# Last quarter of the output stage of a decoder layer: ScalarE and GpSimd in written order, weight columns two tiles ahead and gates one tile ahead

## The chip, the core and the metric

The kernel is one program on one core of a Trainium2 chip. Its time is the device time of one execution in microseconds (us); lower is better. The core's engines have queues of their own and each runs its queue in order: TensorE (PE in the rows, its weight loads PEld), VectorE (DVE), ScalarE (ACT), GpSimd (POOL) and SyncE (SP), which issues most of the DMAs. GpSimd issues DMAs too, from the same queue as its arithmetic.

## What is computed

One decoder layer on 2048 tokens of width 1024, in float32. Cut to the part around the change:

```python
y_a = sliding_window_attention(...) @ w_attn_out     # (T, 512) @ (512, 1024)
y_b = gated_delta_rule(...)         @ w_dn_out       # (T, 512) @ (512, 1024)
merged = sigmoid(g_a) * y_a + sigmoid(g_b) * y_b
x = layer_norm(ALPHA * x + merged @ w_out)
x = layer_norm(ALPHA * x + square(relu(x @ w_up)) @ w_down)
```

## The kernel before, in words

**Stages.** A first stage projects the input and runs attention and the delta rule, and leaves in DRAM the two mixer outputs (`ya_d`, `yb_d`) and tanh of half the gates (`tg_d`). Then comes the output stage, the one that the change touches (about 1166 to 1533 us of the execution). An up stage (L1403 is its matmul) and a down stage (L1525) follow. Every matmul operand is split in a high and a low part, so a product takes three matmuls per block of 128.

**The output stage** runs over four quarters of 512 tokens (`q`, L1021). A quarter has two halves:

- The column half, L1029 to L1066: eight tiles `m` of 128 output columns. `y_weights(m)` (L1008) loads the columns `m` of both weights through SP (L1015, L1016) and splits them on ScalarE (L110, high part) and VectorE (L111, low part). Two products of 12 matmuls each (L147) fill one PSUM bank each out of six. VectorE multiplies each bank with (1 + gate) (L1063), adds the two (L1064), ScalarE rounds the sum to the high part `mgh` (L1065) and VectorE takes the low part `mgl` (L1066). The two gate tiles of `m` come by two DMAs of GpSimd (L1035) into a ring of six places, so a load for tile `m` waits until tile `m`-3 has been used up.
- The row half, L1089 to L1112: `merged @ w_out` for four blocks of 128 rows (matmul L1110), with the residual added by VectorE (L1112).

**What rides along.** The four row blocks of quarter `q` are normalised during the column half of quarter `q`+1, one each at `m` = 1 to 4 (L1046 to L1049): statistics on VectorE (L872 to L876), the reciprocal root on GpSimd (L877), two passes on VectorE (L881, L883), and a store that GpSimd issues (L884). Three tiles later, at `m` = 4 to 7, the block is transposed (`turn_rows`, L1000): eight transposes on PE (L1004) into two PSUM banks, two copies out on ScalarE (L1006) into two buffers `xt`, two stores that GpSimd issues (L1007). PE's order is the order of the program text throughout.

**In the last quarter only**, `x_sums` (L894) prepares the first half of the up stage's input: four chunks of 1 MB, each a load that GpSimd issues (L899), four subtractions on GpSimd (L888, L889, L891, L892) and a store that GpSimd issues (L902). Two steps of it are taken per tile (L1055 to L1057): the first step ends the chunk before (L891, L892, store) and issues the next load, the second does L888 and L889 on what that load brings. After the column half the row loads (L1078) and the first operands of the up stage (L946, L951, L954) are issued.

**What sets the order.** Outside a `manual_schedule` region, a planner at compile time orders each engine's queue by its own model of readiness and by priority. Inside a region, the engines named keep the order of the program text. PE is in one from the start; the row half of the last quarter has one for VectorE and ScalarE (L1081); the up and down stages have one for VectorE, ScalarE, GpSimd and SP. The column half has none for ScalarE and GpSimd, so the planner may put loads, sums and roots where it likes.

```python
            for m in range(NK):
                gates = []
                for i in range(2):
                    th = tgs[:, tgn % 6, :]
                    tgn += 1
                    if q > 0 or m > 2:
                        lastg = G.dma_start(th, tg_d[q][:, i * NK + m, :])
                    gates.append(th)
...
                if lastq:
                    next(sums, None)
                    next(sums, None)
                wh, wl = wy or y_weights(m)
```

Of the kernel before, what the change touches and what calls it, by code (L numbers as in the profile page):

```python
# [10 lines left out]
AF = mybir.ActivationFunctionType  # L11
ALU = mybir.AluOpType
# [3 lines left out]
P = 128  # L16
T = 2048
D = 1024
NK = D // P
TQ = 512  # L20
# [25 lines left out]
def hybrid_layer(ctx: ExitStack, tc: tile.TileContext, x, w_in, conv_w, sinks, a_log, dt_bias, norm_w,  # L46
                 w_attn, w_dn, w_out, ln1_g, ln1_b, w_up, w_down, ln2_g, ln2_b, out):
    nc = tc.nc
    V, A, G, PE = nc.vector, nc.scalar, nc.gpsimd, nc.tensor
# [103 lines left out]
    with ExitStack() as st:  # L153
# [4 lines left out]
        ps = pool(st, "a_ps", space=PSUM)  # L158
# [705 lines left out]
    def layer_norm(*args, **kw):  # L864
        for _ in norm_steps(*args, **kw):
            pass
# [102 lines left out]
    with ExitStack() as st:  # L969
        sb = pool(st, "b_sb")  # L970
        ps = pool(st, "b_ps", space=PSUM)

        def prepare(q):
            ys = []
            for i, src in enumerate((ya_d[q], yb_d[q])):
                t = xslot(2 * (q % 2) + i)
                yh, yl = t[:, 0], t[:, 1]
                for hf in range(2):
                    hs = slice(2 * hf, 2 * hf + 2)
                    raw = stage[:, 2 * i + hf]  # L980
                    if q == 0:
                        with tc.high_priority(offset=HP):
                            loads.append(nc.sync.dma_start(raw, src[:, hs, :]))
                    else:
                        G.dma_start(raw, src[:, hs, :])
                    split(raw, yh[:, hs, :], yl[:, hs, :])
                ys.append((yh, yl))
            return ys

        stage = xslot(5, (4, 2, TQ), F32)  # L990
        turned = []
        loads = []
        ready = prepare(0)
        V.memset(mh, -0.5)
        tgs = xslot(4, (8, TQ), F32)
        tgn = 0

        def turn_rows(r, t):

            s, th, tb = t // 8, t // 4 % 2, t % 4  # L1000
            for kh in range(2):
                ps_ = acc_bank((P, 4, P))
                for k in range(4):
                    PE.transpose(ps_[:, k, :], r[:, (kh * 4 + k) * P:(kh * 4 + k + 1) * P], ident)  # L1004
                xt = new(sb, [P, 4, P], "xt", 2)
                A.activation(xt, ps_, AF.Copy)  # L1006
                G.dma_start(x1t_d[s][:, kh, th, :, tb * P:tb * P + P], xt)  # L1007

        def y_weights(m):
            ms = slice(m * P, (m + 1) * P)  # L1010

            def load_y(raw):
                wa = w_attn.rearrange("(j t d) c -> j d t c", j=2, t=4)
                for j in range(2):
                    nc.sync.dma_start(raw[64 * j:64 * j + 64, 0:4, :], wa[j][:, :, ms])  # L1015
                loads.append(nc.sync.dma_start(raw[:, 4:8, :], w_dn[:, ms].rearrange("(k p) c -> p k c", p=P)))  # L1016

            with (tc.issue_after(loads[-1].ins) if len(loads) < 20 else nullcontext()):
                return weights(None, [NK, P], load=load_y)

        for q in range(NQ):  # L1021
            t0 = q * TQ
            ys = ready
            lastq = q == NQ - 1
            mgh = xslot(6, (NK, TQ))
            mgl = new(sb, [P, NK, TQ], "mgl", 1, F32R)
            if q == NQ - 1:
                sums = x_sums(0, lambda c: stage[:, 2 * (c % 2):2 * (c % 2) + 2].rearrange("p a b t -> p (a b) t"), TQ)
            for m in range(NK):  # L1029
                gates = []  # L1030
                for i in range(2):
                    th = tgs[:, tgn % 6, :]
                    tgn += 1
                    if q > 0 or m > 2:
                        lastg = G.dma_start(th, tg_d[q][:, i * NK + m, :])  # L1035
                    gates.append(th)
                wy = y_weights(m) if q == 0 else None
                if q == 0 and m < 3:
                    with tc.issue_after(loads[-1].ins):
                        for i, th in enumerate(gates):  # L1040
                            loads.append(nc.sync.dma_start(th, tg_d[q][:, i * NK + m, :]))
                if q == 0 and m == 6:
                    with tc.issue_after(lastg.ins):
                        G.dma_start(gt, ln1_g[0].partition_broadcast(P))
                        G.dma_start(bt_, ln1_b[0].partition_broadcast(P))
                if m > 0 and norms:  # L1046
                    r, t = norms.pop(0)
                    layer_norm(r, gt, bt_, mh, x1_d[t])
                    turned.append((r, t, m + 3))  # L1049
                if turned and turned[0][2] <= m:  # L1050
                    turn_rows(*turned.pop(0)[:2])
                if m == 4 and not lastq:
                    with tc.issue_after(lastg.ins):
                        ready = prepare(q + 1)
                if lastq:  # L1055
                    next(sums, None)
                    next(sums, None)  # L1057
                wh, wl = wy or y_weights(m)
                for i in range(2):
                    yh, yl = ys[i]  # L1060
                    pp = new(ps, [P, TQ], "b", 6)
                    product(pp, wh, wl, [yh], [yl], 4, 4 * i)
                    V.scalar_tensor_tensor(gates[i], gates[i], 1.0, pp, ALU.add, ALU.mult)  # L1063
                V.tensor_tensor(gates[0], gates[0], gates[1], ALU.add)  # L1064
                A.activation(mgh[:, m, :], gates[0], AF.Copy, scale=0.5)  # L1065
                V.scalar_tensor_tensor(mgl[:, m, :], gates[0], 0.5, mgh[:, m, :], ALU.mult, ALU.subtract)  # L1066
            while turned:
                turn_rows(*turned.pop(0)[:2])
            early = iter(("B11", "T1", "T2", "T3", "B21")) if lastq else iter(())
            ne = 0  # L1070
            if lastq:
                for _ in sums:
                    pass
            rt = []
            for tb in range(4):
                r = row_tile()
                with tc.issue_after(lastg.ins):
                    G.dma_start(r, rows(t0 + tb * P))  # L1078
                rt.append(r)

            with tc.manual_schedule(engines={V.engine, A.engine}) if lastq else nullcontext():  # L1081
                def out_weights(n):
                    ch, kk = divmod(n, 4)
                    cs = slice(ch * 512, ch * 512 + 512)
                    return weights(w_out[kk * 256:kk * 256 + 256, cs].rearrange("(k p) c -> p k c", p=P), [2, 512])

                ready_w = [out_weights(0), out_weights(1)]
                begun = []
                for ch in range(2):  # L1089
                    cs = slice(ch * 512, ch * 512 + 512)  # L1090
                    accs = [new(ps, [P, 512], "b", 6) for _ in range(4)]
                    for kk in range(4):
                        wh, wl = ready_w.pop(0)
                        if ch * 4 + kk + 2 < 8:
                            ready_w.append(out_weights(ch * 4 + kk + 2))
                        for steps in begun:
                            run(steps)
                        begun = []
                        name = next(early, None)
                        if name:  # L1100
                            with tc.issue_after(lastg.ins):
                                begun.append(x_operand(0, name, xops[0], [flat(stage[:, 2 * (ne % 2) + i]) for i in range(2)], G))
                                next(begun[0])
                            ne += 1
                        for tb in range(4):
                            ts_ = slice(tb * P, tb * P + P)
                            for k in range(2):
                                kg = 2 * kk + k
                                for n, (a, b) in enumerate(((mgh, wh), (mgh, wl), (mgl, wh))):
                                    PE.matmul(accs[tb], lhsT=a[:, kg, ts_], rhs=b[:, k, :], start=kg == 0 and n == 0, stop=kg == 7 and n == 2)  # L1110
                    for tb in range(4):
                        V.scalar_tensor_tensor(rt[tb][:, cs], rt[tb][:, cs], ALPHA, accs[tb], ALU.mult, ALU.add)  # L1112
            for tb in range(4):
                norms.append((rt[tb], q * 4 + tb))
# [472 lines left out]
```

## Time and profile before

| | |
|---|---|
| median of three runs | 2804.24 us (2802.61 to 2807.36) |
| the profiled execution's own time | 2804.84 us |
| its span, first to last instruction | 2803.1 us |
| PE busy over the span | 2736.3 us (98%) |
| VectorE, ScalarE, GpSimd busy | 1910.8, 1198.7, 691.5 us |
| column half of the last quarter | 1435.0 to 1489.3 us |

The rows of the profile further down are of a few kinds. A timeline row gives the start in us, the duration in us, the engine, the line, the operation, what is written and read, how many instructions were merged, and in brackets how long the engine was idle before and what ended that. A windows row gives a stretch and, for each engine, its busy time and instructions, then the granted TensorE clock as a share of full speed, the DMA engines' busy share and GB/s. A source view is about one line of the kernel: its instructions with minimum, median and maximum duration in ns, who waited for them, and for a DMA the time from issue to landing.

### The profile page before, as it was taken

The page shows a single profiled execution, that of the slowest core. Times are in us where ns is not written, and L with a number is a line of the kernel's source. Part 1 is how long each engine was busy: PE and PEld are TensorE (multiplying, and loading weights), DVE is VectorE, ACT ScalarE, POOL GpSimd, SP SyncE. Part 2 cuts the span into 40 slices and gives each one's busy share as a digit, 9 for nine tenths or more (in the row PEclk, how much of TensorE's full clock was granted, in tenths as well). Part 3 has the DMA queues.
Part 4 walks back from the last instruction along what each step waited for, and adds up shares of the span by engine and source line. Part 5 has one row for each costly group of instructions (what it writes and reads, how often), then busy time and mean ns, then how long its engine had stood idle before and what let it go on. Part 6 is the DMA issues. An engine that isn't in the chain of part 4 may idle for free.

```text
span 2803.1 us, 37882 instructions
## 1 busy us (share of the span) xinstructions
PE 2736.3 (98%) x13509; PEld 2258.8 (81%) x13509; DVE 1910.8 (68%) x3034; ACT 1198.7 (43%) x2400; POOL 691.5 (25%) x915
## 2 busy tenths in 40 slices
PE   8999999999999999999999999999999999999996
PEld 6878888888888888888878888878887788888875
DVE  6875666456636673566757866688866777777778
ACT  4545443444344434433324555565555332223344
POOL 1022302230223032213452124458830000000015
PEclk9999999999999999999999999999999999999998
DMA  6785546444635464867787677788976644444443
GB/s 215 233 278 192 210 169 213 136 176 169 211 133 192 158 202 143 235 214 266 251 275 254 192 225 233 245 284 296 301 240 210 233 157 148 132 133 148 146 143 139
DMA packets 356045, 569.92 MB, mean 203 GB/s; under 512 B 42273, under 2 KB 236945, under 8 KB 355857
## 3 DMA queue, kind: packets, MB, share of 16 engines
q1 hardware_dynamic: 315056, 428.54, 47.1%
q0 software_dynamic: 40800, 138.96, 14.2%
q8 instruction: 107, 1.75, 0.3%
q14 instruction: 82, 0.66, 0.1%
HBM read 391.22 MB, written 176.19 MB: 202 GB/s over the span
## 4 chain that ended last, share of the span: by engine, by line
PE 83%; DVE 7%; DMA 4%; issue 2%; ACT 2%; POOL 1%; SPq 0%; DVEq 0%; ACTq 0%; POOLq 0%
PE pj L329 25%; PE X L1403 12%; PE X L1525 11%; PE Z L1403 6%; PE Z L1525 5%; PE b L1110 5%; PE b L147 5%; PE Y L1403 3%; PE Y L1525 3%; PE d L554 2%; DMA w<-in_w_in_dram 1%; DVE prod L542 1%; DVE qs L543 1%; PE at L779 1%; PE d L488 1%
## 5 line engine op out<-in xcount | busy, mean ns | idle before, releaser
L329 PE MATMUL pj<-x,w 128*128 128x512 f32 x3648 | 930.3, 399 | 4.6 <-DVE qs L723 2.1
L329 PEld LDWEIGHTS pj<-x,w 128*128 128x128 f32 x3648 | 662.1, 189 | 129.0 <-issue 2.5
L1525 PE MATMUL X<-x,w 128*128 128x512 f32 x1536 | 370.1, 394 | 11.9 <-DVE st L1487 7.8
L1403 PE MATMUL X<-x,w 128*128 128x512 f32 x1536 | 366.6, 391 | 6.2 <-ACT c L1359 5.0
L1525 PEld LDWEIGHTS X<-x,w 128*128 128x128 f32 x1536 | 290.0, 190 | 77.4 <-issue 15.0
L1403 PEld LDWEIGHTS X<-x,w 128*128 128x128 f32 x1536 | 288.7, 188 | 68.3 <-ACT c L1359 6.3
L1232 ACT ACTIVATE w<-w 128x1024 fp32r<-128x1024 f32 x96 | 101.5, 1059 | 258.9 <-DMA w<-h 253.6
L1403 PE MATMUL Z<-x,w 128*128 128x512 f32 x768 | 184.9, 390 | 0.0
L1525 PE MATMUL Z<-x,w 128*128 128x512 f32 x768 | 184.5, 389 | 0.0
L1146 DVE TENSOR_TENSOR w<-w,w 128x512 fp32r<-128x512 f32 x224 | 175.4, 794 | 9.2 <-ACT w L1142 9.2
L147 PE MATMUL b<-x,w 128*128 128x512 f32 x768 | 179.9, 393 | 0.5 <-DVE x L1063 0.5
L111 DVE TENSOR_TENSOR w<-w,w 128x1024 fp32r<-128x1024 f32 x102 | 125.7, 1232 | 79.8 <-PE b L1110 44.7
L110 ACT ACTIVATE w<-w 128x1024 fp32r<-128x1024 f32 x102 | 107.8, 1057 | 161.4 <-DMA w<-in_w_dn_out_dram 90.9
L147 PEld LDWEIGHTS b<-x,w 128*128 128x128 f32 x768 | 144.0, 189 | 30.7 <-DVE x L1063 0.9
L1525 PEld LDWEIGHTS Z<-x,w 128*128 128x128 f32 x768 | 144.1, 188 | 29.9
L1403 PEld LDWEIGHTS Z<-x,w 128*128 128x128 f32 x768 | 143.9, 188 | 29.9
L1475 DVE SCALAR_TENSOR_TENSOR x<-x,X 128x1024 f32<-128x1024 f32 x96 | 117.0, 1219 | 62.3 <-PE X L1525 62.3
L1110 PE MATMUL b<-w,x 128*128 128x512 f32 x512 | 157.6, 389 | 0.0
L1142 ACT ACTIVATE w<-w 128x512 fp32r<-128x512 f32 x224 | 135.9, 621 | 48.3 <-DVE w L1152 26.8
L1488 POOL TENSOR_TENSOR st<-st,mh 128x1 f32<-128x1 f32 x12 | 6.5, 552 | 580.8 <-DVE st L1487 580.8
L1236 DVE TENSOR_TENSOR w<-w,w 128x1024 fp32r<-128x1024 f32 x96 | 123.0, 1282 | 13.6 <-ACT w L1232 13.5
L414 DVE SCALAR_TENSOR_TENSOR acc<-cin,cw,acc 128x512 f32<-128x512 f32 x144 | 114.8, 797 | 15.9 <-ACT acc L412 13.6
(326 smaller groups left out, 4351.4 us busy)
## 6 DMA issues: line engine op xcount, KB each, us to landing
w<-whd SPq DMA_DIRECT2D x114, 512.0 KB, 3.3
w<-wld SPq DMA_DIRECT2D x114, 512.0 KB, 4.6
h<-c SPq DMA_DIRECT2D x224, 256.0 KB, 4.3
w<-h SPq DMA_DIRECT2D x96, 512.0 KB, 3.5
w<-in_w_up_dram SPq DMA_DIRECT2D x64, 512.0 KB, 5.8
w<-in_w_in_dram SPq DMA_DIRECT2D x38, 512.0 KB, 4.4
whd<-w SPq DMA_DIRECT2D x38, 512.0 KB, 3.0
wld<-w SPq DMA_DIRECT2D x38, 512.0 KB, 5.0
```

The source lines that it names most:

```text
L110: A.activation(hi, raw, AF.Copy)
L111: V.tensor_tensor(lo, raw, hi, ALU.subtract)
L147: PE.matmul(pp, lhsT=a[:, k0 + k, :], rhs=b[k // 4][:, k % 4, :], start=n == 0, stop=n == 3 * nk - 1)
L329: PE.matmul(pp, lhsT=a[:, k, :], rhs=b[k // 4][:, k % 4, :], start=n == 0, stop=n == 23)
L414: V.scalar_tensor_tensor(acc, cin[:, j:j + TQ], cw[:, 12 * j + gi:12 * j + gi + 1], acc, ALU.mult, ALU.add)
L1110: PE.matmul(accs[tb], lhsT=a[:, kg, ts_], rhs=b[:, k, :], start=kg == 0 and n == 0, stop=kg == 7 and n == 2)
L1142: A.activation(t[:, 0, :], src, AF.Copy)
L1146: V.tensor_tensor(l, raw[name], h, ALU.subtract)
L1236: V.tensor_tensor(parts[1], raw_, parts[0], ALU.subtract)
L1403: PE.matmul(dst, lhsT=l[:, ks], rhs=r[:, xs], start=first and k == 0 and m == 0, stop=k == 3 and m == 2, skip_group_check=not first)
L1475: V.scalar_tensor_tensor(dst, dst, 1.0 if (tq, half, ch) in touched else ALPHA, bank, ALU.mult, ALU.add)
L1525: PE.matmul(dst[:, j], lhsT=l[:, ks], rhs=r[:, k], start=first and k == 0 and m == 0, stop=k == 1 and m == 2, skip_group_check=not first)
```

## The change

In the last quarter alone the column half is put in a `manual_schedule` region for ScalarE and GpSimd, so that both keep the order of the program text there, DMA issues of GpSimd included. To suit that order, `y_weights` is written two tiles ahead and the gate loads one tile ahead. No operation is added or taken away. The other quarters keep their text and the planner's order.

```diff
-            for m in range(NK):
+            def load_gates(m):
+                nonlocal tgn, lastg
                 gates = []
                 for i in range(2):
                     th = tgs[:, tgn % 6, :]
...
                         lastg = G.dma_start(th, tg_d[q][:, i * NK + m, :])
                     gates.append(th)
+                return gates
+
+            with tc.manual_schedule(engines={A.engine, G.engine}) if lastq else nullcontext():
+                coming = [y_weights(0), y_weights(1)] if lastq else []
+                gates_of = [load_gates(0)] if lastq else []
+                for m in range(NK):
+                    if lastq:
+                        if m + 1 < NK:
+                            gates_of.append(load_gates(m + 1))
+                        gates = gates_of.pop(0)
+                    else:
+                        gates = load_gates(m)
...
+                    if m > 0 and norms:
+                        r, t = norms.pop(0)
+                        layer_norm(r, gt, bt_, mh, x1_d[t])
+                        turned.append((r, t, m + 3))
+                    if turned and turned[0][2] <= m:
+                        turn_rows(*turned.pop(0)[:2])
...
+                    if lastq:
+                        next(sums, None)
+                        next(sums, None)
+                    if lastq:
+                        if m + 2 < NK:
+                            coming.append(y_weights(m + 2))
+                        wy = coming.pop(0)
+                    wh, wl = wy or y_weights(m)
...
+                        V.scalar_tensor_tensor(gates[i], gates[i], 1.0, pp, ALU.add, ALU.mult)
+                    V.tensor_tensor(gates[0], gates[0], gates[1], ALU.add)
+                    A.activation(mgh[:, m, :], gates[0], AF.Copy, scale=0.5)
+                    V.scalar_tensor_tensor(mgl[:, m, :], gates[0], 0.5, mgh[:, m, :], ALU.mult, ALU.subtract)
```

## Rows read from the trace of the kernel before

**Rows 1.** Windows view, this column half: PE, PEld, DVE, ACT, POOL, clock, DMA.
```profile
1435.00:1489.30 54.30, 49.41 (x226) 40.46 (x225) 39.65 (x54) 16.41 (x22) 32.58 (x39) 0.97 0.86 277
```

**Rows 2.** The chain that ended last: eight tiles of the first quarter without a pause.
```profile
1165.94 43.58 PE b L147 x192
```

**Rows 3.** Timeline of PE in the last quarter's column half.
```profile
1435.00 19.25 PE L147 MATMUL b<-x,w 128*128 128x512 f32 x84
...
1468.48 1.56 PE L1004 MATMUL pj<-ident,r 128*128 128x128 f32 x8 [4.38 <-ACT xt L1006]
1469.69 7.04 PE L147 MATMUL b<-x,w 128*128 128x512 f32 x24
...
1482.94 1.04 PE L1004 MATMUL pj<-ident,r 128*128 128x128 f32 x8
1483.73 5.69 PE L147 MATMUL b<-x,w 128*128 128x512 f32 x24
1489.26 0.61 PE L1110 MATMUL b<-w,x 128*128 128x512 f32 x2
```

**Rows 4.** Timeline of VectorE around the first row block's normalisation.
```profile
1434.44 0.15 DVE L876 TENSOR_SCALAR rs<-mv 128x1 f32<-128x1 f32 x1
...
1449.17 1.28 DVE L883 SCALAR_TENSOR_TENSOR r<-r,rs,lnb 128x1024 f32<-128x1024 f32 x1 [6.97 <-POOL rs L877]
1450.37 0.68 DVE L1063 SCALAR_TENSOR_TENSOR x<-x,b 128x512 f32<-128x512 f32 x1
```

**Rows 5.** Timeline of GpSimd: the later chunks of the sums, the first root.
```profile
1425.20 0.78 POOL L899 DMA_DIRECT2D x<-x1t  x1 [1.68 <-DMA xsum<-x]
...
1434.27 1.29 POOL L888 TENSOR_TENSOR x<-x 128x512 f32<-128x512 f32 x1 [4.66 <-DMA x<-x1t]
1435.65 2.14 POOL L889 TENSOR_TENSOR x<-x 128x512 f32<-128x512 f32 x1
...
1444.86 1.28 POOL L891 TENSOR_TENSOR x<-x 128x512 f32<-128x512 f32 x1
...
1447.80 0.75 POOL L902 DMA_DIRECT2D xsum<-x  x1 [0.30 <-POOL x L892]
1448.49 0.64 POOL L877 TENSOR_TENSOR rs<-rs,mh 128x1 f32<-128x1 f32 x1
1450.75 0.60 POOL L884 DMA_DIRECT2D x<-r  x1 [1.62 <-DVE r L883]
```

**Rows 6.** Source view of L899 alone: the load issued at 1425.20.
```profile
DMA to landing us min/median/max: 9.0/9.0/9.0
```

**Rows 7.** Source view of L899 over the whole execution.
```profile
  POOL r L888: 46.5, 8
DMA to landing us min/median/max: 4.9/7.6/12.7
```

**Rows 8.** Timeline of GpSimd in the up stage, in written order there.
```profile
1675.70 0.78 POOL L899 DMA_DIRECT2D r<-x1t  x1
1682.38 1.03 POOL L888 TENSOR_TENSOR r<-r 128x256 f32<-128x256 f32 x1 [5.90 <-DMA r<-x1t]
```

**Rows 9.** Source view of L1035, the gate loads, 1450 to 1482.
```profile
L1035 POOL DMA_DIRECT2D x<-tg x10: 538/556/581, 1456.8 to 1479.3; - x10
```

**Rows 10.** Source view of L1007, stores of the turned rows, 1460 to 1500.
```profile
L1007 POOL DMA_DIRECT2D x1t<-xt x8: 760/766/778, 1468.7 to 1490.3; - x8
DMA to landing us min/median/max: 3.5/5.5/8.0
```

**Rows 11.** Windows view, PE's stretch after the longest pause of this half.
```profile
1468.50:1477.00 8.50, 8.50 (x36) 7.05 (x37) 8.47 (x13) 2.97 (x5) 6.11 (x9) 0.80 0.83 278
```

**Rows 12.** Timeline of ScalarE: the row half's first split among the column half's work.
```profile
1464.32 1.06 ACT L110 ACTIVATE w<-w 128x1024 fp32r<-128x1024 f32 x1 [1.41 <-DVE w L111]
1467.32 0.63 ACT L1065 ACTIVATE x<-x 128x512 fp32r<-128x512 f32 x1 [1.94 <-DVE x L1064]
```

**Rows 13.** Source view of L902 alone: the 1 MB store issued at 1442.71.
```profile
DMA to landing us min/median/max: 5.0/5.0/5.0
```

More of the change, by code (lines that the diff above doesn't have):

```diff
@@ L996, in hybrid_layer @@
         tgn = 0
+        lastg = None
         def turn_rows(r, t):
@@ L1036, in hybrid_layer @@
                     gates.append(th)
[L1037 to L1066, printed above, removed]
+                return gates
@@ new lines, in hybrid_layer @@
+            with tc.manual_schedule(engines={A.engine, G.engine}) if lastq else nullcontext():
[8 more added lines that the diff above has]
+                        gates = load_gates(m)
+                    wy = y_weights(m) if q == 0 else None
+                    if q == 0 and m < 3:
+                        with tc.issue_after(loads[-1].ins):
+                            for i, th in enumerate(gates):
+                                loads.append(nc.sync.dma_start(th, tg_d[q][:, i * NK + m, :]))
+                    if q == 0 and m == 6:
+                        with tc.issue_after(lastg.ins):
+                            G.dma_start(gt, ln1_g[0].partition_broadcast(P))
+                            G.dma_start(bt_, ln1_b[0].partition_broadcast(P))
+                    if m > 0 and norms:
[4 more added lines that the diff above has]
+                        turn_rows(*turned.pop(0)[:2])
+                    if m == 4 and not lastq:
+                        with tc.issue_after(lastg.ins):
+                            ready = prepare(q + 1)
+                    if lastq:
[6 more added lines that the diff above has]
+                    wh, wl = wy or y_weights(m)
+                    for i in range(2):
+                        yh, yl = ys[i]
+                        pp = new(ps, [P, TQ], "b", 6)
+                        product(pp, wh, wl, [yh], [yl], 4, 4 * i)
+                        V.scalar_tensor_tensor(gates[i], gates[i], 1.0, pp, ALU.add, ALU.mult)
+                    V.tensor_tensor(gates[0], gates[0], gates[1], ALU.add)
+                    A.activation(mgh[:, m, :], gates[0], AF.Copy, scale=0.5)
+                    V.scalar_tensor_tensor(mgl[:, m, :], gates[0], 0.5, mgh[:, m, :], ALU.mult, ALU.subtract)
```

## The prediction

> **What bounds the kernel now.** I read the windows of the output stage first, then PE's timeline in the last quarter's column half, then the queues that PE turns out to wait for. The half lasts from 1435.00 to 1489.26, 54.26 us [rows 1, 3]. Its matmuls need less: eight tiles of the same size without a pause took 43.58 us in the first quarter [rows 2], and four groups of transposes take 0.79 us each (from the start at 1482.94 to the product's start at 1483.73 [rows 3]). That is 46.7 us, so 7.5 us are pauses and slow matmuls, and no more than that can be won here. The largest pause, 4.38 us, has PE's transposes waiting for ScalarE to empty their bank, and the tile behind it takes 7.04 us where the last one takes 5.69 [rows 3], at a granted clock of 0.80 [rows 11], so part of that stretch ran at the 1.2 GHz level.
>
> The pause has its root in GpSimd. VectorE had the first row block's variance ready at 1434.6 (1434.44 and 0.15 us), but stood idle 6.97 us before L883, which needs the root L877 [rows 4]. GpSimd computed that root only at 1448.49, behind two chunks of the sums, whose first subtraction began at 1434.27 [rows 5]. VectorE carried the lost time along as a backlog. So now the planner hides two chunks' loads in the quarter before, and pays with one late root.
>
> **What the change does, part by part.** *GpSimd's order* is the part that counts. No instruction is added, but GpSimd's queue must now run as the text stands, per tile: two gate loads for the next tile, root L877, store L884, turned rows' stores L1007, then the end of the old chunk (L891, L892, store L902), the load L899 of the new chunk, and at once L888 on what that load brings. Nothing stands between L899 and L888, so GpSimd waits out the whole landing time of a 1 MB load at `m` = 1, 2 and 3. The load at `m` = 0 can still be early. The next ones cannot, for they now stand behind the root of `m` = 1, and that root needs the row sums that VectorE has only at 1434.6 [rows 4]. A load issued at 1425.20 [rows 5] moves behind it. Queued behind each wait are the next tile's gates, the next root and the stores that free `xt`; VectorE, ScalarE and PE wait for those.
>
> The up stage shows this pattern already, since GpSimd keeps written order there: it waited 46.5 us for eight loads of the sums [rows 7], for example 5.90 us after the load issued at 1675.70 and until 1682.38 [rows 8]. There nothing else needed GpSimd. Here gates, roots and transposes do.
>
> One round, from root to root, costs:
>
> - root to the end of issuing L884: 1448.49 to 1451.35 (1450.75 and 0.60), 2.86 us [rows 5]. VectorE was waiting then, as it will be.
> - L891, L892 and the store's issue: 1444.86 to 1448.55 (1447.80 and 0.75), 3.69 us [rows 5].
> - the load to its landing: 9.0 us, from the one load of this size issued at 1425.20 [rows 6]. The bounds are 4.9 and 12.7, the shortest and longest of all twelve loads on this line [rows 7]; the lower end is from the 512 KB ones of the up stage. The 1 MB store landed in 5.0 [rows 13]. I take 9.0, because the 512 KB load of rows 8, issued right behind a store as these will be, took 6.7 us (1682.38 less 1675.70), and this one is twice as large.
> - L888 and L889: twice 1.29 us and about 0.1 between them, 2.7 us [rows 5]. Beside a busy VectorE one took 2.14 [rows 5], so up to 0.85 us more for each of the four subtractions of a round, 10 us over three rounds at the very worst.
> - two gate loads: twice 0.556 us, 1.1 us [rows 9].
>
> That is 19.35 us a round. Three rounds put the root of `m` = 4 at 1434.6 + 58.05 = 1492.65. After it L884 ends 2.86 later at 1495.5; the two stores L1007, which start 0.77 us apart, land 5.5 us after issue [rows 10], at 1501.0 and 1501.8. Only then may ScalarE fill `xt` with the next turned rows (0.6 us each, so 1502.4) and free the bank for the transposes of `m` = 6. Those end at 1502.8. Product 6 takes 5.55 us, plus 1.3 us for the slow clock after a pause (7.04 less 5.69, [rows 3]), to 1509.7. The next transposes take 0.79 and product 7 takes 5.55, to 1516.05. (The second group of turned rows is not later: the end of the last chunk, 3.69, and gates, 1.1, let L1007 go at 1501.8, landing at 1507.3 and 1508.1, copied out by 1508.7.) The row half then starts at 1516.05 in place of 1489.26: **26.8 us later**. Of this, 27.0 us are the three landings, and all else together is worth about nothing against the 7.5 us of old pauses.
>
> The Trainium skill, page "DMA: Bandwidth & Descriptors", section on the anatomy of one DMA on the GpSimd path, fits a fixed 2.0 us plus the bytes at 436 GB/s, which makes an estimated 4.4 us for 1 MB. With it the sum would be 3 x 4.6 us smaller, 13 us in place of 26.8. The trace does not agree in this stage: 9.0 us [rows 6], with the DMA engines 0.86 busy over the half [rows 1].
>
> *ScalarE's order* I cost at nothing. The turned rows' copies stood early or late in its queue only as VectorE's backlog placed them; in written order the copies of `m` = 4 stand behind the rounding of tile 3, which by the times above is done before PE needs it. *Columns two tiles ahead:* a split of 1.06 us [rows 12] and its low part then have about 10.9 us of PE work (two tiles of 43.58 / 8 [rows 2]) to hide under; without that cover it would be some 2.1 us per tile (twice 1.06, the low part taken as long as the split), but PE is idle long before that matters. *Gates one tile ahead* would help if GpSimd were free; it is in the round above. SP's queue holds the same column loads, none moved past another. *The row half* keeps its length: its row loads and first operands follow the last gate load, which goes out at about 1505, earlier against the row half than today.
>
> **Sum.** The profiled execution took 2804.84 us, 0.6 above the median of 2804.24. Median plus 26.8 is **2831.0 us**, 0.95% slower.
>
> **The rivals.**
>
> - *Short landings.* With few other transfers under way while PE stands still, the loads may land like the 1 MB store, in 5.0 us [rows 13]. For it: fewer loads overlap than today. Against: the landings of [rows 6, 8]. Three times 4.0 less: 2819 us. (The Trainium skill's fit, cited above, would make it some 2817 us.)
> - *ScalarE holds the row half back as well.* If the planner puts the first split of `w_out` behind the last rounding of the column half, PE waits after product 7 for two VectorE operations of 0.68 us [rows 4], the rounding of 0.63, the split of 1.06 [rows 12] and its low part, taken as long, some 4.1 us. Against: today that split, at 1464.32, stands ahead of the rounding of tile 2 at 1467.32, though its region is another [rows 12], so the two orders mix freely. 2835 us.
> - *Not slower: GpSimd's waits stay covered.* This needs the written order to leave the DMA issues alone, so that the loads still go out ahead of the roots; then roots come when VectorE asks, the 7.5 us vanish, and the time is 2804.2 - 7.5 = 2796.7 us. The point that decides is the landing time that GpSimd sees: the sum above is three landings less 0.2, so it ends equal only if a 1 MB load is seen for under 0.1 us, and within 0.2% (5.6 us, about what a measurement of this kernel can tell from no change) under 1.9 us. No load on this line landed under 4.9 [rows 7]. Against it also: the up stage's waits, where issues on GpSimd did keep their place [rows 7, 8].
>
> **How the numbers follow.** The forecast gets 0.73, short landings 0.11, the held row half 0.07; these are all slower, 0.91. Of the 0.09 for covered waits, 0.05 is faster, and 0.04 is for loads half covered, within 0.2%. The range: landings of 5.0 in place of 9.0 take 12 us off, and 2.5 more for an earlier first root and short gaps gives 2816. Landings of 12.7 add 11.1, and a third of the worst contention on the subtractions adds 3.3, which gives 2845. The held row half lies inside. What is left out is the not-slower case and a tail above.
>
> **What would show it.** Right: in the changed profile GpSimd waits three times, 5 to 10 us each, at L888 for `x<-x1t` between 1435 and 1495; the roots L877 lie 16 to 23 us apart; PE has one pause of 25 to 35 us before the transposes of `m` = 6, put down to ScalarE's copies or behind them L1007; VectorE no longer idles 7 us at 1442; L1110 of the last quarter starts near 1516; the up and down stages keep their lengths. Wrong: the loads L899 of chunks 1 to 3 go out before the first root, or the roots lie 6 us apart, or the half ends before 1490.

## The result, and the profile after

The changed kernel takes 2826.14 us (median of four runs, 2821.08 to 2829.96) against 2803.71 for the kernel before on the same chip: a ratio of 1.008, 95% interval 1.0066 to 1.0094, or 22.4 us slower. The profiled execution took 2826.71 us, with a span of 2825.0. In this profile the lines below L1000 are shifted: the gate loads are L1037, the transposes L1005, the turned rows' copies and stores L1007 and L1008, the work behind the products (gates, sum, rounding, low part) L1082 to L1085, the row half's matmul L1129 and its residual L1131.

The windows of the last quarter, first after the change (the column half, PE's two long pauses in it, the row half), then the row half of the kernel before (its column half is [rows 1]); columns as in [rows 1]:

```profile
1432.09:1507.70 75.61, 51.42 (x226) 42.18 (x225) 43.56 (x57) 16.55 (x23) 43.49 (x47) 0.84 0.72 242
1466.70:1483.05 16.35, 0.01 (x1) 0.00 (x0) 5.88 (x8) 1.23 (x2) 7.65 (x10) 0.59 0.56 209
1491.60:1499.10 7.50, 0.03 (x2) 0.01 (x1) 3.66 (x4) 1.60 (x3) 5.49 (x5) 0.85 0.86 306
1507.70:1555.40 47.70, 45.08 (x193) 36.92 (x192) 30.04 (x35) 18.89 (x23) 7.87 (x14) 0.96 0.65 223
```

```profile
1489.30:1532.80 43.50, 43.50 (x194) 36.02 (x193) 31.05 (x37) 19.44 (x24) 6.33 (x11) 1.00 0.64 222
```

The column half went from 54.26 to 75.57 us (1432.09 to 1507.66), the row half from 43.52 to 47.77 (to 1555.43, where the up stage begins). Together that is 25.6 us. The half began 2.9 us earlier in this execution and what follows it took 0.75 less, which leaves the 21.9 us by which the span grew. Over all profiles of this study the half begins anywhere from 1431.4 to 1439.2, so only lengths of stages are compared below, each from the one execution that was profiled.

PE's timeline of the last quarter after the change, which answers to [rows 3]:

```profile
1432.09 21.93 PE L147 MATMUL b<-x,w 128*128 128x512 f32 x96
...
1460.98 5.73 PE L147 MATMUL b<-x,w 128*128 128x512 f32 x24
1483.05 1.12 PE L1005 MATMUL pj<-ident,r 128*128 128x128 f32 x4 [16.34 <-ACT xt L1007]
...
1485.31 6.31 PE L147 MATMUL b<-x,w 128*128 128x512 f32 x24
1499.10 1.97 PE L1005 MATMUL pj<-ident,r 128*128 128x128 f32 x8 [7.47 <-ACT xt L1007]
1500.71 7.11 PE L147 MATMUL b<-x,w 128*128 128x512 f32 x24
1507.66 0.62 PE L1129 MATMUL b<-w,x 128*128 128x512 f32 x2
...
1534.92 1.22 PE L1129 MATMUL b<-w,x 128*128 128x512 f32 x2 [2.62 <-DVE r L1131]
```

Up to the product of `m` = 5 PE runs without a pause. Then it waits 16.34 us in front of the transposes of `m` = 6 and 7.47 us in front of those of `m` = 7, both times for ScalarE to copy out the transposes before, and once more inside the row half. Behind the two long pauses the products take 6.31 and 7.11 us in place of 5.73 (the granted clock over the half is 0.84, a mixture of the two levels 1.2 and 2.4 GHz).

Why ScalarE could not copy is on GpSimd's timeline, which answers to [rows 5]:

```profile
1431.77 1.53 POOL L877 TENSOR_TENSOR rs<-rs,mh 128x1 f32<-128x1 f32 x1 [21.09 <-DVE rs L876]
...
1440.10 0.79 POOL L899 DMA_DIRECT2D x<-x1t  x1
...
1443.66 0.57 POOL L877 TENSOR_TENSOR rs<-rs,mh 128x1 f32<-128x1 f32 x1
...
1448.60 1.37 POOL L888 TENSOR_TENSOR x<-x 128x512 f32<-128x512 f32 x1 [0.64 <-DMA x<-x1t]
1450.05 2.97 POOL L889 TENSOR_TENSOR x<-x 128x512 f32<-128x512 f32 x1
...
1459.06 0.61 POOL L877 TENSOR_TENSOR rs<-rs,mh 128x1 f32<-128x1 f32 x1
...
1461.86 0.78 POOL L899 DMA_DIRECT2D x<-x1t  x1
1472.43 1.26 POOL L888 TENSOR_TENSOR x<-x 128x512 f32<-128x512 f32 x1 [9.79 <-DMA x<-x1t]
1473.77 1.25 POOL L889 TENSOR_TENSOR x<-x 128x512 f32<-128x512 f32 x1
...
1476.10 0.57 POOL L877 TENSOR_TENSOR rs<-rs,mh 128x1 f32<-128x1 f32 x1
...
1478.87 0.78 POOL L1008 DMA_DIRECT2D x1t<-xt  x1
...
1485.17 0.78 POOL L899 DMA_DIRECT2D x<-x1t  x1
...
1487.02 1.52 POOL L1008 DMA_DIRECT2D x1t<-xt  x2
1493.07 1.26 POOL L888 TENSOR_TENSOR x<-x 128x512 f32<-128x512 f32 x1 [4.53 <-DMA x<-x1t]
...
1510.74 1.05 POOL L946 DMA_DIRECT2D x<-x1t  x2
```

The first turned rows were ready in `xt` at 1459.1, but their store L1008 was issued at 1478.87. In between GpSimd's queue held, in the order of the text, the root of 1459.06 and its store, a load of the sums, 9.79 us of waiting for that load, two subtractions, two gate loads, the next root and its store. The second pair of stores went out at 1487.02, behind the third such load. ScalarE's timeline shows the copies waiting for these stores (the third row is the split of a `w_out` block that waits for its own load):

```profile
1458.07 1.07 ACT L1007 ACTIVATE xt<-pj 128x512 f32<-128x512 f32 x2
...
1482.40 0.60 ACT L1007 ACTIVATE xt<-pj 128x512 f32<-128x512 f32 x1 [14.14 <-DMA x1t<-xt]
...
1497.50 1.06 ACT L110 ACTIVATE w<-w 128x1024 fp32r<-128x1024 f32 x1 [9.65 <-DMA w<-in_w_out_dram]
1498.46 1.07 ACT L1007 ACTIVATE xt<-pj 128x512 f32<-128x512 f32 x2
```

Source views of the same half: the store L1008 issued at 1480.80, the two issued at 1487.02 and 1487.8, and the three 1 MB loads of L899.

```profile
DMA to landing us min/median/max: 2.7/2.7/2.7
...
DMA to landing us min/median/max: 9.6/9.8/9.9
...
DMA to landing us min/median/max: 7.8/8.4/10.5
```

The first pair of stores landed in 3.5 us (the one of 1478.87, by the same view) and 2.7 us, so the first pause comes from their late issue. The second pair landed at about 1497, and the split of 1497.50 let the copies go at 1498.46. So the second pause is the slow landing of two stores, and about 1 us of it is ScalarE's own order.

### The profile page after: what moved, and what is told of

The parts are those of the page before. It is cut to its first block, busy times and chain, and to the rows that moved or that the text cites. A ratio compares the mean times of both kernels' runs of the same rounds, so it can differ in the third digit from the quotient of the medians.

```text
span 2825.0 us, 37863 instructions
## 1 busy us (share of the span) xinstructions
PE 2735.8 (97%) x13509; PEld 2258.2 (80%) x13509; DVE 1919.1 (68%) x3034; ACT 1197.1 (42%) x2400; POOL 694.2 (25%) x915
## 3 DMA queue, kind: packets, MB, share of 16 engines
q1 hardware_dynamic: 315056, 428.54, 46.8%
## 4 chain that ended last, share of the span: by engine, by line
PE 81%; DVE 7%; DMA 5%; issue 3%; POOL 2%; ACT 1%; SPq 0%; DVEq 0%; POOLq 0%; ACTq 0%
PE pj L329 25%; PE X L1422 12%; PE X L1544 11%; PE Z L1422 6%; PE Z L1544 5%; PE b L1129 5%; PE Y L1422 3%; PE Y L1544 3%; PE d L554 2%; PE b L147 2%; DMA x<-x1t 1%; DMA w<-in_w_in_dram 1%; DVE prod L542 1%; DVE qs L543 1%; PE at L779 1%
## 5 line engine op out<-in xcount | busy, mean ns | idle before, releaser
L1129 PE MATMUL b<-w,x 128*128 128x512 f32 x512 | 158.9, 392 | 2.9 <-DVE r L1131 2.6
```

## The experiments

**Which engine's order costs the time?** Three kernels keep the changed text and alter only the region's list of engines.

GpSimd alone:

```diff
-            with tc.manual_schedule(engines={A.engine, G.engine}) if lastq else nullcontext():
+            with tc.manual_schedule(engines={G.engine}) if lastq else nullcontext():
```

> The column half's region names GpSimd alone; ScalarE goes back to the planner. Theory G (the price is GpSimd's queue: the landings of the sums' loads, waited out in front of gates, roots and the stores that free xt): still 15 to 25 us slower than before, 2819 to 2829 us, with the long pauses of PE before the transposes. Theory S (the price is ScalarE's written order, which puts the copies of turned rows behind roundings and lets a split of w_out wait for its load in front of them): the pauses go and the time is 2800 to 2806 us.

Measured: 2826.35 us, ratio 1.0083 (1.0058 to 1.0109), as much as the whole change and inside Theory G's range. PE's pauses in its column half:

```profile
1484.61 2.31 PE L1005 MATMUL pj<-ident,r 128*128 128x128 f32 x8 [17.12 <-ACT xt L1007]
1498.41 1.97 PE L1005 MATMUL pj<-ident,r 128*128 128x128 f32 x8 [4.31 <-ACT xt L1007]
```

ScalarE alone (`engines={A.engine}` in the same line):

> The column half's region names ScalarE alone; GpSimd goes back to the planner, which may send the sums' loads out early again. Theory G: at most 5 us from before, 2799 to 2809 us. Theory S: 2815 us or more, with PE waiting for ScalarE's copies. A share of both: 2809 to 2815 us.

Measured: 2809.54 us, ratio 1.0024 (1.0009 to 1.0039), half a microsecond above Theory G's range and inside the one for a share of both. The long pauses are gone, but PE waits for a split of columns, though it is written two tiles ahead. PE's timeline, then ScalarE's:

```profile
1455.87 0.73 PE L147 MATMUL b<-x,w 128*128 128x512 f32 x2 [3.95 <-ACT w L110]
```

```profile
1454.24 0.63 ACT L1084 ACTIVATE x<-x 128x512 fp32r<-128x512 f32 x1 [28.28 <-DVE x L1083]
```

ScalarE stood 28.28 us at the rounding of a tile for which VectorE was late, and the split, at 1454.78, stood behind it in written order. VectorE was late because it had stood 9.55 us for the first root, which GpSimd, in the planner's order here, computed at 1446.69 behind two chunks of the sums, as in [rows 5].

No region at all (`with nullcontext():` in the same line), so that only the places in the text differ from the kernel before:

> No region in the column half; columns are still written two tiles ahead and gates one tile ahead. Theories G and S both: as before within 5 us, 2799 to 2809 us. If instead the new places in the text cost the time by themselves (the priority that the planner gives each instruction comes from them), 2815 us or more.

Measured: 2804.97 us, ratio 1.0005 (0.9991 to 1.0018). The places in the text alone cost nothing that these runs can tell. GpSimd's order carries the price; ScalarE's is worth about 6 us by itself, beside that late root, and nothing that can be told on top of GpSimd's.

**Is it the waiting for the sums' loads?** This kernel leaves out the four 1 MB loads of `x_sums(0)`, and so a part of the computation; the subtractions run on what lies in the buffers.

```diff
-            G.dma_start(t, x1t_d[s].rearrange("p a b k t -> p (a b) (k t)")[:, :, cs])
+            if s == 1:
+                G.dma_start(t, x1t_d[s].rearrange("p a b k t -> p (a b) (k t)")[:, :, cs])
```

> The changed kernel without the four 1 MB loads of the first half's sums; the subtractions and stores stay and work on what lies in the buffers, so the sums that the up stage reads are other numbers. Theory G: GpSimd's waits in front of L888 (0.64, 9.79 and 4.53 us in the changed kernel's trace) are gone, the pause of 16.3 us before the transposes of tile 6 shrinks by about 10 and the later one by some 4, so 2809 to 2815 us. What stays over before's 2804 us is GpSimd's own work in written order and ScalarE. Theory S: the loads do not matter, 2822 to 2830 us.

Measured: 2811.6 us, ratio 1.0025 (1.0013 to 1.0037), as Theory G expected. The column half takes 55.55 us, 20 less than with the loads, and within 1.3 of the kernel before. The row half takes 49.93, so what is left of the price lies there. These are PE's pauses, the last one in the row half:

```profile
1468.68 1.27 PE L1006 MATMUL pj<-ident,r 128*128 128x128 f32 x8 [1.89 <-ACT xt L1008]
1479.57 2.07 PE L1006 MATMUL pj<-ident,r 128*128 128x128 f32 x8 [2.69 <-ACT xt L1008]
1522.39 1.22 PE L1130 MATMUL b<-w,x 128*128 128x512 f32 x2 [3.67 <-DVE r L1132]
```

Without the loads their traffic is gone too, so the 20 us are not all waiting. The first pair of `xt` stores was issued 34.9 us after the start of the half, in place of 46.8, which is mostly the waiting. The second pair (issued at 1481.34) landed in 4.9 us, in place of 9.6 and 9.9, which may be the traffic; no run separates the two.

The next one keeps the loads but takes one step fewer at two tiles, so that the loads of the last two chunks have the next tile's gates, root and stores behind them in the queue instead of their own subtractions.

```diff
-                        next(sums, None)
+                        if m not in (3, 5):
+                            next(sums, None)
```

> The changed kernel with one step of the sums fewer at tiles 3 and 5, so that the loads of chunks 2 and 3 both have the next tile's gates, root and stores behind them in GpSimd's queue and not their own subtractions. In the changed kernel chunk 2 alone was followed at once by its subtractions and waited 9.79 us. Theory G: that wait shrinks to 1 to 4 us, the gates of tile 5, the root of tile 4 and the stores that free xt come some 7 us earlier, PE's pause of 16.3 us shrinks to 5 to 10: 2814 to 2821 us. If another cause set that pause (ScalarE's order, the weights): 2823 to 2830 us.

Measured: 2822.54 us, ratio 1.0069 (1.0054 to 1.0084), between the two expectations; PE's pause before `m` = 6 fell to 11.57 us, not to 5 to 10. GpSimd's timeline of it, then a row of VectorE's:

```profile
1464.03 0.78 POOL L899 DMA_DIRECT2D x<-x1t  x1
...
1465.89 0.57 POOL L877 TENSOR_TENSOR rs<-rs,mh 128x1 f32<-128x1 f32 x1
1472.76 0.59 POOL L884 DMA_DIRECT2D x<-r  x1 [6.30 <-DVE r L883]
1473.34 0.77 POOL L1008 DMA_DIRECT2D x1t<-xt  x1
...
1476.04 1.28 POOL L888 TENSOR_TENSOR x<-x 128x512 f32<-128x512 f32 x1
```

```profile
1465.62 0.69 DVE L1083 SCALAR_TENSOR_TENSOR x<-x,b 128x512 f32<-128x512 f32 x1 [1.86 <-DMA x<-tg]
```

The wait for the third chunk's load is gone, but the queue now stands 6.30 us at L884, for VectorE. VectorE came to L883 only at 1471.18, since it had waited, 1.86 and then 1.26 us, for two gate tiles that landed 5.4 and 8.0 us after their issue (from 1460.1 on), right behind a 1 MB store of the same queue. The store of `xt` left at 1473.34 instead of 1478.87, and the column half shrank by 6.3 us to 69.26. In a queue kept in order, a wait that is taken away lets the next one show.

**Do two buffers `xt` set the pauses?** The changed kernel with a third one:

```diff
-                xt = new(sb, [P, 4, P], "xt", 2)
+                xt = new(sb, [P, 4, P], "xt", 3)
```

> The changed kernel with three buffers xt in place of two. Theory G (the stores that free xt are issued late, because GpSimd waits 9.8 us at L888 for the third chunk): a third buffer gives PE only one more group of four transposes, so the pause of 16 us stays at 13 to 16 us (perhaps moved between the two groups of m = 6), the later one of 7.5 us shrinks to 2 to 6, 2820 to 2825 us. Rival (two buffers are too few, and the loads' waits matter little): both pauses fall under 3 us, 2803 to 2810 us.

Measured: 2826.85 us, ratio 1.0087 (1.0069 to 1.0105), the price of the change unaltered, above the expected 2820 to 2825. PE's pauses add up to 21.1 us, in place of 23.8 (16.34 and 7.47), and only lie elsewhere:

```profile
1470.31 1.12 PE L1005 MATMUL pj<-ident,r 128*128 128x128 f32 x4 [4.25 <-ACT xt L1007]
1483.30 1.12 PE L1005 MATMUL pj<-ident,r 128*128 128x128 f32 x4 [11.87 <-ACT xt L1007]
1497.51 1.11 PE L1005 MATMUL pj<-ident,r 128*128 128x128 f32 x4 [4.96 <-ACT xt L1007]
```

The lateness of the stores decides, not the number of buffers.

**Where does the longer row half come from?** VectorE's timeline in the changed kernel's row half: the low part of an operand of the up stage (L954) waits for ScalarE, and L1131, for which PE waits at 1534.92, stands behind it in written order.

```profile
1533.05 1.23 DVE L954 TENSOR_TENSOR x<-x,x 128x1024 fp32r<-128x1024 f32 x1 [2.35 <-ACT x L951]
1534.19 2.47 DVE L1131 SCALAR_TENSOR_TENSOR r<-r,b 128x512 f32<-128x512 f32 x4
```

The loads of those operands, L946, stood behind the last stores of the turned rows in GpSimd's queue. Issued by SP instead:

```diff
-begun.append(x_operand(0, name, xops[0], [flat(stage[:, 2 * (ne % 2) + i]) for i in range(2)], G))
+begun.append(x_operand(0, name, xops[0], [flat(stage[:, 2 * (ne % 2) + i]) for i in range(2)], nc.sync))
```

> The changed kernel with the row half's loads of the up stage's first operands (L946) issued by SP, not by GpSimd behind the last stores of the turned rows. Theory (the row half's 47.8 us in place of 43.5 come from operands that arrive late, VectorE's L954 in front of L1131): the row half takes 43.5 to 45.5 us, and the total is 2821 to 2824. Rival (it comes from elsewhere, residual rows or the order of VectorE): 47 to 48 us, 2825 to 2828.

Measured: 2820.47 us, ratio 1.0066 (1.0046 to 1.0085), half a microsecond under the expected range. The windows view of its row half has PE busy throughout:

```profile
1507.80:1551.35 43.55, 43.55 (x194) 36.07 (x193) 30.80 (x36) 16.90 (x21) 2.63 (x4) 1.00 0.68 246
```

43.52 us from its first matmul to the up stage, exactly the kernel before. (By the ratios the total fell by 0.14%, 3.9 us; the two intervals overlap, so the window is the clearer evidence.) The other profiles agree: where ScalarE's first L951 starts 9.6 us or less after the row half, the half takes 43.5 us; at 11.0 to 13.0 us it takes 44.9, at 14.9 to 15.7 us 48.2 to 49.9. The changed kernel, at 12.5 us and 47.77, is the one that lies off this line. The column half keeps the changed kernel's text here and yet took 72.50 in place of 75.57, so a difference of 3 us between the column halves of two single executions shows little.

**Is there an order that beats both?** One idea writes the sums ahead of the loop: two whole chunks and two loads before the first root, then one step per tile from `m` = 2. Its core, with the region for both engines:

```diff
+                ts = [move(0, True), move(1, True)]
+                for c in range(2):
+                    for _ in block_sums(ts[c]):
+                        pass
+                    move(c, False)
+                for c in range(2, 4):
+                    move(c, True)
...
-                    if lastq:
-                        next(sums, None)
+                    if lastq and m > 1:
                         next(sums, None)
```

> Both engines in written order as in the changed kernel, but the text of the sums is other: chunks 0 and 1 whole and the loads of chunks 2 and 3 are written ahead of the tile loop, so they run beside the row half of the quarter before; in the loop from tile 2 on one step per tile, subtractions and stores only. No load is left in front of a root. Theory G: the 22 us go, 2798 to 2808 us, roots about one tile apart. If written order itself is dear, whatever the place of the loads: 2813 us or more.

Measured: 2809.12 us, ratio 1.0022 (1.0011 to 1.0034). The same text with the region for GpSimd alone:

> As the run with the sums ahead, but the region names GpSimd alone and ScalarE is the planner's. Written order of ScalarE alone cost 6 us beside the planner's GpSimd. If that is ScalarE's order as such, this is 3 to 6 us faster than with both: 2796 to 2804 us. If it came from that run's own GpSimd order, no difference beyond 3 us.

Measured: 2806.94 us, ratio 1.0021 (1.0008 to 1.0033). And with no region:

> The text with the sums ahead, no region. Shows what the planner makes of it: if it only follows readiness, as before within 4 us (2800 to 2808 us), with two chunks' subtractions in front of the first root again; if the text's place moves the roots ahead of the subtractions, 2796 to 2800 us.

Measured: 2805.28 us, ratio 1.0002 (0.9993 to 1.0011). The last is as expected, with two chunks in front of the first root again (1448.44). The first missed both its ranges. The second came out as if ScalarE's order made no difference: 2.2 us from the first by the medians, 0.0001 by the ratios. So the 6 us of ScalarE's order alone seem to hang on the planner's late root beside it. Writing the sums ahead takes 16 of the 22 us away. GpSimd no longer waits for the sums (timeline of the second), the first root comes when VectorE asks, but the second stands behind gate loads that wait for a place in their ring:

```profile
1432.59 1.53 POOL L877 TENSOR_TENSOR rs<-rs,mh 128x1 f32<-128x1 f32 x1 [4.22 <-DVE rs L876]
...
1444.88 1.09 POOL L1059 DMA_DIRECT2D x<-tg  x2 [7.36 <-DVE mgl L1109]
1445.99 1.42 POOL L877 TENSOR_TENSOR rs<-rs,mh 128x1 f32<-128x1 f32 x1
```

So gates written one tile ahead may have a price of their own, which the loads' waits covered in the changed kernel. This is argued from the rows, not shown: gates written behind the root were not tried.

The other idea leaves the planner its freedom and takes away only the late root of the kernel before: the subtractions of the third and fourth chunk may be issued only after the latest root (`roots` collects what L877 returns). It was run with two and with three buffers `xt`.

```diff
+            if s == 0 and c > 1:
+                with tc.issue_after(roots[-1].ins):
+                    for _ in block_sums(t):
+                        pass
+                yield
+            else:
+                yield from block_sums(t)
```

> The kernel before (planner's order, no region, gates and columns as they were), with one edit: the subtractions of the third and fourth chunk of the sums may be issued only after the latest root L877. Loads and stores stay as they are. Theory G (the late root of the kernel before, 1448.49 behind two chunks of sums, is what feeds its 4.38 us pause of PE): VectorE's idle of 7 us goes, the pause shrinks, 2797 to 2801 us, and the column half takes 47 to 51 us. Rival (the two xt buffers and the landing of their stores set the pause, whatever the root does): 2802 to 2806 us, a pause of 3 us or more for ACT xt stays.

> The same edit as the one beside it (subtractions of the third and fourth chunk behind the latest root) with three buffers xt for the turned rows in place of two. If the root feeds the pause: as the kernel beside it, 2797 to 2801, the third buffer worth under 1 us. Rival (two xt buffers set the pause): 2796 to 2800 here, where the kernel with two stays at 2802 to 2806.

Measured: 2807.28 us with two buffers, ratio 1.0016 (1.0003 to 1.003), and 2804.53 with three, 1.0 (0.9989 to 1.0011). With two, GpSimd's and PE's timelines:

```profile
1434.53 1.53 POOL L879 TENSOR_TENSOR rs<-rs,mh 128x1 f32<-128x1 f32 x1 [6.14 <-DVE rs L878]
```

```profile
1477.43 1.35 PE L1012 MATMUL pj<-ident,r 128*128 128x128 f32 x8 [0.91 <-ACT xt L1014]
1511.45 0.73 PE L1118 MATMUL b<-w,x 128*128 128x512 f32 x2 [2.73 <-DVE r L1120]
```

The root comes 14 us earlier than in [rows 5], the 4.38 us pause of [rows 3] is gone, and the column half takes 49.22 us in place of 54.26, all as Theory G had it. But here the planner put the first operand loads behind the last stores of the turned rows, 6.0 us after the row half began (1490.06 against 1484.08), and that half took 48.18: what one half won, the other gave back. The median lies above both named ranges, 4.5 us over the kernel before by the ratio, and the two halves do not explain that rest. With three buffers the halves took 51.00 and 43.51, 3.3 us less than the kernel before in the two profiles. But that profile is of the fastest of twelve executions (2797.99), and the median lies above both expected ranges and shows no gain. No kernel run here beats the kernel before.

| kernel | column half, us | row half, us | ratio |
|---|---|---|---|
| before | 54.26 | 43.52 | 1 |
| changed | 75.57 | 47.77 | 1.0080 |
| GpSimd's order alone | 74.61 | 44.90 | 1.0083 |
| ScalarE's order alone | 57.98 | 43.52 | 1.0024 |
| no region | 52.40 | 43.52 | 1.0005 |
| no sum loads | 55.55 | 49.93 | 1.0025 |
| loads a tile ahead | 69.26 | 48.45 | 1.0069 |
| changed, three `xt` | 74.43 | 48.28 | 1.0087 |
| operands by SP | 72.50 | 43.52 | 1.0066 |
| sums ahead, both engines | 58.18 | 44.93 | 1.0022 |
| sums ahead, GpSimd | 58.16 | 44.90 | 1.0021 |
| sums ahead, no region | 54.83 | 43.52 | 1.0002 |
| sums behind roots | 49.22 | 48.18 | 1.0016 |
| same, three `xt` | 51.00 | 43.51 | 1.0000 |

## Why the prediction was right, and where its steps failed

**The cause was right.** GpSimd's queue in written order, standing at L888 for loads of the sums in front of roots, gates and the stores that free `xt`: with that order alone the whole price is there, and without the loads (and their traffic) the column half is back within 1.3 us. PE's long pause came where it was put, before the transposes of `m` = 6, but with 16.34 us it was shorter than the 25 to 35 forecast. The direction holds, and 2826.14 lies 4.9 us under the forecast. Its other signs came out in part: one wait of three is in its 5 to 10 us, one round of three in its 16 to 23, and a second pause of PE stands beside the one it named.

**The step that failed is the reading of the sums' steps.** The prediction, and the account of the kernel above it, have two steps per chunk, the first of which ends one chunk and issues the next load, so that each of three loads is followed at once by its own L888. But L894 yields once more behind the store: a chunk is three steps (load; L888 and L889; L891, L892 and the store), taken two per tile. Written out, the tiles get: load and first half of chunk 0; its second half and load 1; both halves of chunk 1; load 2 and its first half; second half and load 3; both halves of chunk 3. Of loads 1 to 3 only load 2 is directly followed by its own subtractions. The other two have a tile's gates, root and stores behind them, which cover part of the landing.

**So the term "three landings of 9.0" was mis-sized, though each landing was not.** The loads landed in 7.8, 8.4 and 10.5 us, mean 8.9. GpSimd saw 0.64, 9.79 and 4.53 of that, 15.0 us, not 27.0, and only the first two, 10.4 us, ahead of the root of `m` = 4; the third came behind the second pair of stores, so it delayed none of the stores that PE's two long pauses waited for. The round of 19.35 us from root to root measured 11.9, 15.4 and 17.0 (1431.77, 1443.66, 1459.06, 1476.10), and the root of `m` = 4 came at 1476.10, not 1492.65 (2.9 us of the difference are the earlier start of the half). So the 9.0 of [rows 6] stood up. The Trainium skill's fit in "DMA: Bandwidth & Descriptors", section on the anatomy of one DMA on the GpSimd path, gives an estimated 4.4 us for 1 MB; the trace does not agree, since no load of this half came near it.

**Two later terms failed the other way.** The prediction let the second pair of turned rows' stores land in 5.5 us ([rows 10]) and found them "not later". They landed in 9.6 and 9.9 us, issued 2.5 us behind a 1 MB store and 1.9 us behind a 1 MB load, and gave the second pause of 7.47 us. Product 6 began at 1485.31, 17.5 us earlier than predicted (the 2.9 included), but from there to the row half it took 22.35 us in place of 13.25. That gives back 9.1 of the 17.5, and the column half ends at 1507.66, not 1516.05.

**"The row half keeps its length" was wrong by 4.25 us.** The prediction had the first operands go out earlier against the row half than today. They went out 3.1 us after its start (1510.74 against 1507.66), where the kernel before issued them 6 us ahead of it (1483.29 against 1489.26), because in written order they stand behind the last stores L1008, which waited for ScalarE. Moving them to SP brought 43.52 back.

**ScalarE's order at nothing** holds for the change as a whole, since GpSimd's order alone costs as much. By itself, beside the planner's late root, that order is worth some 6 us, which was not foreseen: the prediction gave the split of columns 10.9 us of PE's work as cover, and did not count that in written order the split stands behind a rounding that waits for VectorE, 28.28 us there.

**The sum held because these errors cancel, which is luck.** Forecast were +26.8 us, all in the column half (54.26 to 81.05); measured were +21.3 there and +4.25 in the row half, 25.6 together. That the medians differ by only 22.4 stays open; the start of the half, 2.9 us earlier in the profile, is not steady from run to run.

**The rivals.** *Short landings* is out: no 1 MB load landed under 7.8 us, and the waits were short for another reason. *ScalarE holds the row half back* named a price of 4.1 us, close to the 4.25 measured, but not its place: a `w_out` split did stand ahead of the copies at 1497.50, worth about 1 us, and the row half's own loss is the operand loads. *Not slower* needed covered waits; one of 9.79 us in the middle of the half was enough against it. What the prediction took for the most that can be won, 7.5 us, was not passed: the best column half, 49.22, recovers 5.0 of it in one execution.

## What to carry to other kernels

When an in-order queue both issues a load and computes on it, write out the queue by hand, instruction by instruction, yields included, before costing it: what stands between the load and its first use decides how much of the landing is seen, and here one chunk in three paid it whole. Price each wait by what stands behind it in that queue: 10.4 us of waiting stood ahead of the stores that free two buffers, and the column half grew by 21.3 us, since the slow landing of the second pair came on top. Follow the delay into the next stage too: loads issued at the end of the queue come late by as much as the queue does, and moving them to another queue brought the row half's whole 4.25 us back.

## What was not expected of the hardware

The same 256 KB store from GpSimd landed in 2.7 us while PE stood still (issued at 1480.80) and in 9.6 to 9.9 us some six us later, behind a 1 MB store and a 1 MB load of the same queue. Which of the two made it slow, or other transfers, no run shows. By the windows and the source views in the section on the result, the DMA engines were 0.56 busy over the first pause and 0.86 over the second. The Trainium skill's fit (same page and section as above) gives an estimated 2.6 us for 256 KB, which the store of 1480.80 matches and the later two do not; the fit is for one DMA.

GpSimd's subtraction of 128x512 took 1.25 us at 1473.77, where VectorE did nothing, and 2.97 at 1450.05, where VectorE was busy for 2.87 of those 2.97 us. The DMA engines were idle over the one and busy over the other, but they are not the reason: the subtraction of 1493.07 took 1.26 us with them 0.99 busy and VectorE 0.04 us. The Trainium skill, "GPSIMD Engine Reference", section on specifications, says that the two share their SBUF interfaces; the trace agrees that one slows beside the other, by a factor of 2.4 here. It is not always GpSimd: the subtraction L891 of 1435.57 took 1.30 us with VectorE busy throughout, and there VectorE's L881 took 2.05 us in place of 1.27. The 2.97 us are more than the 2.14 of [rows 5], from which the prediction bounded the four subtractions of a round.
